# A hybrid decoder layer: the out-projection's rank in the schedule, and half buffers for its transposed rows

## The chip, the cores and the metric

The kernel runs on one core of one Trainium2 chip. The metric is the device time of one execution in microseconds (us). The kernel before was timed in three runs; one more execution was taken with the hardware profiler.

## The reference, cut to what matters

One decoder layer works on 2048 prompt rows and 64 sample rows (eight sequences of eight) of width 1024, all sharing the weights:

```python
proj = x @ w_in                       # columns split among three mixers
oa = gated_delta_chunked(...)         # mixer A, 6 heads, chunks of 64
ob = rg_lru(...)                      # mixer B, width 256
oc, gla_new = gla_chunked(qc, kc, vc, logf, st_gla)   # mixer C, 6 heads, chunks of 64
oc = head_rms_norm(oc, norm_c_w) * silu(zc)
heads = concatenate([oa, ob, oc], -1)
x = layer_norm(ALPHA * x + heads @ w_out, ln1_g, ln1_b)
f, fconv_new = conv_ffn(x, st_fconv, ffn_w_up, ffn_conv_w, ffn_conv_b, ffn_w_down)
x = layer_norm(ALPHA * x + f, ln2_g, ln2_b)
```

The change lies where mixer C, the product with `w_out` and the first layer norm are computed.

## The kernel before, in words

The program has four stages. `phase1` computes the columns of `x @ w_in` and stores them in DRAM; `window_a` runs mixer A; `window_c` runs mixer C and the out-projection; `phase3` is the feed-forward part. Products in full precision are made from three products of split operands (`mm3`, line 320): high by high, low by high, high by low.

`window_c` walks over nine groups: the sample rows first (`G[8]`), then eight groups of 256 prompt rows. For each it calls:

- `load` (L1276, L1279): the group's decays, keys, queries and values, on SP's queue. It is called one group ahead.
- `prep`: `natural` and `tokens` make scaled copies and transposes; then for each of six heads `fill` lays out the keys and queries (copies on ACT at L1349 to L1362, 36 small DMAs K<-KN in all for a group on SP's queue at L1351 and L1359, products on GpSimd at L1353 and L1363), and `scores` multiplies them (L1374) and gathers the result in `RC` (a copy at L1377 for the first level, then masked copies at L1380).
- `chain`: four chunks in sequence. Each has state products into `cs` (L1428, copied by L1437 into the next chunk's state) and output products into `po` (L1431). After two chunks `head_norm` turns `po` into the last three rows of `mx`, the heads of a tile of 128 rows. `dest` gets `mx` and the tile's `x` by DMA (L1511, L1513).
- for each tile of 128 rows, the projection `P(t0)`: split `mx` into `mh` (ACT, L1525) and `ml` (GpSimd, L1526), 48 matmuls with `woh` and `wol` into two `pm` banks (L320), `ALPHA * x` added (L1532), layer norm (L1171 to L1186), store of the rows to `s_x1` (L1537). Then `P.transposed` with `keep=1`: for the tile before, eight transposes into two `pm` banks (L1550), two copies into `xt` (ACT, L1551), a store of `xt` to `s_x1T` (SP, L1553).

The sample group has a second half: `sample` reads the eight GLA states into four buffers that `spare()` borrows from the projection's pool, and updates and stores them (L1447 to L1469). Between its two halves `P.weights` loads `w_out` in eight pieces through the ring `x` (L1495) and splits them into `woh` (ACT, L1496) and `wol` (DVE and GpSimd in turn, L1497).

The buffers that couple the two kinds of work: `mx` has two slots, `x` three, `mh`, `ml` and `xt` one each, the `pm` banks two (shared by projection and transposes), the `po` banks two. `RC`, `XC` and `KC` alternate between two groups; fills go through three sets of slots.

The order on each engine in `window_c` is not written out by hand. A scheduler takes the instructions in the order in which the program traces them as their rank, and a ready instruction of better rank goes first. `tc.high_priority(n)` moves the rank of what is in it by `n` places; a negative number is a setback. In the kernel before, `P` and `P.transposed` are set back by 100,000, more than there are instructions in the stage. `phase3` has an order written out by hand; its buffers take the place of those of `window_c`, and it reads `x1T0` (prompt rows up to 1023) first, five of eight pieces by GpSimd's queue and three by SP's (L1667).

Of the kernel before, what the change touches and what calls it, by code (L numbers as in the profile page):

```python
# [8 lines left out]
F32 = mybir.dt.float32  # L9
# [7 lines left out]
T = 2048  # L17
# [4 lines left out]
KD = DM // 128  # L22
# [281 lines left out]
def load_consts(E, pool, names):  # L304
    t = {}
    for n in names:
        o, w = _CST[n]
        t[n] = pool.tile([128, w], F32, name="c_" + n)
        E.nc.sync.dma_start(t[n], E.d["consts"][:, o:o + w])
    return t  # L310
# [1166 lines left out]
class Project:  # L1477
# [21 lines left out]

    def spare(self):  # L1500

        tags = [("mx", 2), ("mh", 1), ("ml", 1), ("xt", 1)]
        return [self.tr.tile([128, 2, 6, 64], F32, tag=t, bufs=b, name="sp" + t) for t, b in tags]

    def dest(self, t0):
# [34 lines left out]
    def transposed(self, ident, keep=0):  # L1540

        E, nc = self.E, self.E.nc
        while len(self.done) > keep:
            t0, m, x = self.done.pop(0)
            xt = self.tr.tile([128, KD, 128], F32, tag="xt", bufs=1, name=f"xt{t0}")
            for j in range(2):
                p = self.pm.tile([128, 4, 128], F32, tag="pm", name=f"pt{t0}{j}")
                for k in range(4):
                    kk = 4 * j + k
                    nc.tensor.transpose(p[:, k], x[:, kk * 128:(kk + 1) * 128], ident)  # L1550
                nc.scalar.copy(xt[:, 4 * j:4 * j + 4], p)  # L1551
            b, o = divmod(t0, 1024) if t0 < T else (1, t0 - 1024)
            nc.sync.dma_start(E.s[f"x1T{b}"].rearrange("(k p) t -> p k t", p=128)[:, :, o:o + m], xt[:, :, :m])  # L1553


def window_c(E):

    with ExitStack() as ctx:
        C = Gla(E, ctx)
        P = Project(E, ctx)  # L1560
        C.C.update(load_consts(E, ctx.enter_context(E.tc.tile_pool(name="c3", bufs=1)), ["ident", "ones"]))
        room = P.spare()
        C.dest = P.dest
        order = [C.G[8]] + C.G[:8]
        C.load(order[0])
        for i, g in enumerate(order):
            if i < 8:
                C.load(order[i + 1])
            C.prep(g)
            if g.smp:  # L1570
                smp = C.sample(g, room)
                next(smp)
                P.weights()
            else:
                if g.g == 0:
                    next(smp)
                C.chain(g)
            for t0 in range(g.t0, g.t0 + g.n, 128):
                with E.tc.high_priority(-10 ** 5):
                    P(t0)  # L1580
                    P.transposed(C.C["ident"], 1)
        P.transposed(C.C["ident"])
# [373 lines left out]
def program(tc, dram):  # L1956

    E = Env()
    E.nc, E.tc, E.d = tc.nc, tc, dram
    with ExitStack() as ctx:  # L1960
        setup(E, ctx)
        phase1(E)
        window_a(E)
        window_c(E)
        phase3(E)
# [16 lines left out]
```

## Time and profile before

| What | Value |
|---|---|
| median of three runs | 3042.56 us (3039.36 to 3044.3) |
| profiled execution, its own time | 3038.56 us |
| span of the profiled execution | 3036.8 us |
| PE busy | 2885.8 us (95%) |
| DVE, ACT, POOL busy | 1521.1, 1230.0, 847.7 us |
| mean granted TensorE clock | 0.954 |
| first score matmul of the sample group, about | 1010 us |
| first and last matmul of the projection | 1096.8 and 1506 us |
| first dense matmul of the feed-forward part | 1508 us |

The profile is one execution. A row of the timeline gives the start in us, the duration, the engine, the line, what is written and read, and how often; in brackets stands the idle time before it and what ended that. A row of a stretch gives busy time by engine, the granted clock of TensorE, the busy share of the DMA engines and GB/s. SPq is SP's queue, which issues almost all DMAs in their order.

### The profile page before, as it was taken

To read this page: it belongs to the slowest core of one execution; us is meant where nothing else is said; L and a number is where in the kernel's file an instruction comes from. 1 tells how busy PE (TensorE), PEld (TensorE's weight loads), DVE (VectorE), ACT (ScalarE), POOL (GpSimd) and SP (SyncE) were. 2 spreads that over 40 slices of the span, in tenths; PEclk is the share of its full clock that TensorE was granted. 3 is DMA by queue.
4 is the path that set the end of the run, shared out by engine and by line. 5 is a ranking of instruction groups with operands and counts; after the bars stand their busy time and mean duration, and the time that the engine had idled before them with its cause. 6 is when DMAs were issued, how large, how long until landed. Compare 5 with 4: busy or idle time off the path is not lost.

```text
span 3036.8 us, 45291 instructions
## 1 busy us (share of the span) xinstructions
PE 2885.8 (95%) x17755; PEld 2497.7 (82%) x17755; DVE 1521.1 (50%) x2454; ACT 1230.0 (41%) x2591; POOL 847.7 (28%) x904
## 2 busy tenths in 40 slices
PE   9999999789889889699899999999999999999998
PEld 8888789678879576577778888888889999999997
DVE  4564442586663777665633333333366444334446
ACT  4474443446653788844332222222232222222223
POOL 0000001734433555533332222222232222222224
PEclk9999999789889589799999999999999999999999
DMA  6221113433433443244531111111124111111111
GB/s 198 81 76 67 58 60 101 137 104 108 119 91 95 114 128 110 83 132 120 184 131 56 49 42 63 42 56 42 49 106 151 42 47 51 49 42 42 47 44 62
DMA packets 196508, 256.77 MB, mean 85 GB/s; under 512 B 43170, under 2 KB 162040, under 8 KB 196232
## 3 DMA queue, kind: packets, MB, share of 16 engines
q1 hardware_dynamic: 194168, 246.58, 26.2%
q0 software_dynamic: 1984, 7.12, 0.6%
q8 instruction: 140, 2.29, 0.3%
q14 instruction: 72, 0.59, 0.1%
q10 hardware_dynamic: 144, 0.20, 0.0%
HBM read 183.94 MB, written 60.08 MB: 80 GB/s over the span
## 4 chain that ended last, share of the span: by engine, by line
PE 78%; DVE 7%; ACT 6%; issue 4%; DMA 3%; POOL 2%; SPq 1%; POOLq 0%; DVEq 0%; ACTq 0%
PE pm L320 19%; PE pd L320 15%; PE pug L320 15%; PE puv L320 15%; PE s L1374 1%; PE zp L1121 1%; DVE Tm L897 1%; DVE y L1789 1%; PE zp L1122 1%; PE zp L1123 1%; ACT Q L1362 1%; ACT WU L920 1%; DVE tmp L895 1%; PE pd L1871 1%; PE cw L962 1%
## 5 line engine op out<-in xcount | busy, mean ns | idle before, releaser
L1725 DVE SCALAR_TENSOR_TENSOR act<-G,cols,act 128x1024 f32<-128x1024 f32 (+1 forms) x132 | 123.6, 951 | 493.0 <-ACT act L1723 490.7
L1878 DVE TENSOR_TENSOR y<-y,pd 128x512 f32<-128x512 f32 x322 | 221.0, 687 | 203.3 <-PE pd L320 196.8
L1616 POOL TENSOR_TENSOR wl_d<-ws_d,wh_d 128x1024 fp32r<-128x1024 f32 x44 | 106.2, 2414 | 571.4 <-ACT wh_d L1615 520.7
L320 PE MATMUL pd<-wh_d,hh 128*128 128x512 f32 x704 | 216.0, 392 | 2.7 <-DVE y L1876 1.8
L320 PE MATMUL pd<-wh_d,hl 128*128 128x512 f32 x704 | 215.3, 391 | 0.0
L320 PE MATMUL pd<-wl_d,hh 128*128 128x512 f32 x704 | 214.9, 390 | 0.0
L1705 ACT COPY G<-pug 128x512 f32<-128x512 f32 (+2 forms) x110 | 55.0, 501 | 386.5 <-PE pug L320 386.5
L320 PE MATMUL pug<-fxh,wh_g 128*128 128x512 f32 (+2 forms) x880 | 196.3, 352 | 2.6 <-ACT wh_g L1615 2.6
L320 PE MATMUL puv<-fxh,wh_v 128*128 128x512 f32 (+2 forms) x880 | 197.2, 353 | 0.8 <-ACT wh_v L1615 0.8
L320 PE MATMUL puv<-fxh,wl_v 128*128 128x512 f32 (+2 forms) x880 | 196.9, 352 | 0.7 <-POOL wl_v L1616 0.7
L320 PE MATMUL puv<-fxl,wh_v 128*128 128x512 f32 (+2 forms) x880 | 196.7, 352 | 0.0
L320 PE MATMUL pug<-fxh,wl_g 128*128 128x512 f32 (+2 forms) x880 | 195.9, 351 | 0.4 <-POOL wl_g L1616 0.4
L320 PE MATMUL pug<-fxl,wh_g 128*128 128x512 f32 (+2 forms) x880 | 195.8, 351 | 0.0
L320 PE MATMUL pm<-xh,wh 128*128 128x448 f32 (+1 forms) x800 | 181.9, 360 | 6.6 <-ACT xh L370 6.4
L1615 ACT CAST wh_d<-ws_d 128x1024 fp32r<-128x1024 f32 x44 | 45.7, 1040 | 339.1 <-PE pd L1871 174.9
L320 PE MATMUL pm<-xh,wl 128*128 128x448 f32 (+1 forms) x800 | 181.5, 358 | 0.0
L320 PE MATMUL pm<-xl,wh 128*128 128x448 f32 (+1 forms) x800 | 179.9, 358 | 0.5 <-DVE xl L371 0.5
L1767 DVE TENSOR_TENSOR hl<-act,hh 128x512 fp32r<-128x512 f32 (+2 forms) x110 | 124.1, 1128 | 99.4 <-ACT hh L1759 99.4
L320 PEld LDWEIGHTS pug<-fxh,wh_g 128*128 128x128 f32 x880 | 156.0, 188 | 17.5 <-ACT wh_g L1615 3.0
L320 PEld LDWEIGHTS puv<-fxh,wh_v 128*128 128x128 f32 x880 | 156.4, 188 | 15.1 <-ACT wh_v L1615 1.2
L320 PEld LDWEIGHTS puv<-fxh,wl_v 128*128 128x128 f32 x880 | 156.1, 188 | 15.0 <-POOL wl_v L1616 1.1
L320 PEld LDWEIGHTS puv<-fxl,wh_v 128*128 128x128 f32 x880 | 156.0, 188 | 13.9
(731 smaller groups left out, 6264.0 us busy)
## 6 DMA issues: line engine op xcount, KB each, us to landing
ws_d<-in_w_dn SPq DMA_DIRECT2D x44, 512.0 KB
ws_g<-in_w_up SPq DMA_DIRECT2D x43, 512.0 KB
ws_v<-in_w_up SPq DMA_DIRECT2D x43, 512.0 KB
zx<-in_xT SPq DMA_DIRECT2D x56, 256.0 KB
ws<-in_w_in SPq DMA_DIRECT2D x19, 512.0 KB
K<-KN SPq DMA_DIRECT2D x288, 32.0 KB
x<-in_x SPq DMA_DIRECT2D x16, 512.0 KB
s_x<-x SPq DMA_DIRECT2D x16, 512.0 KB
```

The lines of the kernel that those rows point to most:

```text
L320: nc.tensor.matmul(ps, w[k], x[k], start=first and i == 0, stop=last and i == 3 * n - 1)
L895: nc.vector.tensor_tensor(t, Y[:, j + 1:, j:j + 1].to_broadcast([128, k, j + 1]), Tm[:, j:j + 1, :j + 1].to_broadcast([128, k, j + 1]), op ...
L897: nc.vector.tensor_tensor(Tm[:, j + 1:, :j + 1], Tm[:, j + 1:, :j + 1], t, op=OP.subtract)
L920: nc.scalar.copy(o[:, h, :, :, jh * 32:(jh + 1) * 32], Ut[r, :, :3 * mt].rearrange("p i (a c) -> p a c i", a=3)[:, :, g.c0:g.c0 + m])
L962: nc.tensor.matmul(ps[64:, h], g.WU[:, h, c], g.X[:, h, c], start=True, stop=True)
L1121: nc.tensor.matmul(ps, wh[:, k], xl, start=k == 0, stop=False)
L1615: nc.scalar.copy(h, t)
L1616: nc.gpsimd.tensor_tensor(lo, t, h.bitcast(F32), op=OP.subtract)
L1705: nc.scalar.copy(G[:, 2 + o:2 + o + m], p[:, :m])
L1725: nc.vector.scalar_tensor_tensor(dst(act), src(i), taps[i], dst(act), op0=OP.mult, op1=OP.add)
L1767: nc.vector.tensor_tensor(dst, act[:, c], hh[:, c].bitcast(F32), op=OP.subtract)
L1878: nc.vector.tensor_tensor(y, y, ps, op=OP.add)
```

## The change

It does three things. The setback of `P` and `P.transposed` goes from 100,000 places to 600. `xt` becomes two half buffers of four blocks each (the pool's default of two buffers), and each half is stored by a DMA of its own right after its copy. `spare()` takes its fourth buffer from the ring `x` (three slots), as the old `xt` is no more.

```diff
     def spare(self):
-        tags = [("mx", 2), ("mh", 1), ("ml", 1), ("xt", 1)]
+        tags = [("mx", 2), ("mh", 1), ("ml", 1), ("x", 3)]
         return [self.tr.tile([128, 2, 6, 64], F32, tag=t, bufs=b, name="sp" + t) for t, b in tags]
...
         while len(self.done) > keep:
             t0, m, x = self.done.pop(0)
-            xt = self.tr.tile([128, KD, 128], F32, tag="xt", bufs=1, name=f"xt{t0}")
+            b, o = divmod(t0, 1024) if t0 < T else (1, t0 - 1024)
             for j in range(2):
+                xt = self.tr.tile([128, 4, 128], F32, tag="xt", name=f"xt{t0}{j}")
                 p = self.pm.tile([128, 4, 128], F32, tag="pm", name=f"pt{t0}{j}")
                 for k in range(4):
                     kk = 4 * j + k
                     nc.tensor.transpose(p[:, k], x[:, kk * 128:(kk + 1) * 128], ident)
-                nc.scalar.copy(xt[:, 4 * j:4 * j + 4], p)
-            b, o = divmod(t0, 1024) if t0 < T else (1, t0 - 1024)
-            nc.sync.dma_start(E.s[f"x1T{b}"].rearrange("(k p) t -> p k t", p=128)[:, :, o:o + m], xt[:, :, :m])
+                nc.scalar.copy(xt, p)
+                nc.sync.dma_start(E.s[f"x1T{b}"].rearrange("(k p) t -> p k t", p=128)[:, 4 * j:4 * j + 4, o:o + m],
+                                  xt[:, :, :m])
...
             for t0 in range(g.t0, g.t0 + g.n, 128):
-                with E.tc.high_priority(-10 ** 5):
+                with E.tc.high_priority(-600):
                     P(t0)
                     P.transposed(C.C["ident"], 1)
         P.transposed(C.C["ident"])
```

## The prediction

> **What bounds the kernel now.** I read the page first (span, chain), then the busy time by stretches of the stage that the change touches, then the timelines of PE, SP and ACT inside the one stretch that looked wrong.
>
> ```profile
> span 3036.8 us, 45291 instructions
> PE 78%; DVE 7%; ACT 6%; issue 4%; DMA 3%; POOL 2%; SPq 1%; POOLq 0%; DVEq 0%; ACTq 0%
> ```
>
> The chain that ends last is TensorE for 78%. A change of order can only help where PE stands still, so I cut the stage of the change (1097 to 1508 us: GLA groups and projection together) into stretches. The columns are PE, PEld, DVE, ACT, POOL busy, then the granted clock.
>
> ```profile
> 1100.00:1220.00 120.00, 112.15 (x1055) 86.98 (x1054) 88.29 (x187) 99.74 (x305) 67.12 (x114) 1.00 0.37 103
> 1220.00:1280.00 60.00, 40.51 (x419) 33.67 (x416) 40.40 (x105) 52.42 (x169) 34.22 (x83) 0.75 0.27 72
> 1280.00:1290.00 10.00, 0.01 (x1) 0.01 (x1) 2.31 (x6) 3.88 (x18) 3.68 (x7) 0.50 0.45 139
> 1290.00:1508.00 218.00, 211.08 (x1347) 166.94 (x1348) 129.71 (x174) 96.22 (x226) 68.45 (x82) 0.98 0.45 139
> ```
>
> Before 1220 PE is busy 112.15 of 120 us (93%) at full clock, after 1290 it is busy 211.08 of 218 (97%). Between lies a hole of 70 us with 40.5 us of PE work at a clock of 0.75 and 0.50. The next rows show why.
>
> ```profile
> 1216.51 0.60 PE L1550 MATMUL pt<-c_ident,x 128*128 128x128 f32 x4
> 1289.99 3.78 PE L320 MATMUL pm<-woh,mh 128*128 128x512 f32 x8 [11.80 <-ACT xt L1551]
> 1191.56 0.58 ACT L1551 COPY xt<-pt 128x512 f32<-128x512 f32 x1
> 1289.35 1.07 ACT L1551 COPY xt<-pt 128x512 f32<-128x512 f32 x2 [3.76 <-DMA s_x1T<-xt]
> 1283.38 2.44 SPq L1351 DMA_DIRECT2D K<-KN  x4
> 1285.88 0.58 SPq L1553 DMA_DIRECT2D s_x1T<-xt  x1
> ```
>
> The second half of one tile's `xt` was copied at 1191.56, yet its store was issued at 1285.88, 94 us later, behind K loads (L1351, L1359) on SP's queue. `xt` is one buffer, so the next tile's transposes, done at 1216.51 into both `pm` banks, could not be copied out before 1289.35. With both banks taken no projection matmul could run. What is left at 1290 shows in the same stretch for the matmuls on `woh` alone:
>
> ```profile
> 1290.00:1508.00 218.00, 110.09 (x416) 79.47 (x416) 0.00 (x0) 0.00 (x0) 0.00 (x0) 0.98 0.45 139
> ```
>
> A tile has 32 of them, so 416 are thirteen of the seventeen tiles, and PE is the bound until they are done. So projection work that moves into the hole shortens the stage almost one for one.
>
> **The change part by part.**
>
> *The rank.* Counting instructions in the code, a group has 397 of its own (load 7, natural 64, tokens 32, six heads of fill and scores at 36, chain 78) and two tiles of projection 144. A setback of 600 puts the projection of group g 59 places behind the same point of group g+1: behind all of g+1's work, ahead of g+2's fills. Today's setback of 100,000 puts it behind everything. The K loads that overtook the store in the hole are fills of later groups; those two or more groups later now rank behind it. I cost the rank as filling the hole. The room in it: the 40.5 us run at a low clock, and the same eight score matmuls show the price of that.
>
> ```profile
> 1209.67 0.68 PE L1374 MATMUL s<-Q,K 128*64 128x64 f32 x8
> 1236.18 1.08 PE L1374 MATMUL s<-Q,K 128*64 128x64 f32 x8 [2.12 <-POOL Q L1353]
> ```
>
> At 0.68 against 1.08 the hole's work is 40.5 x 0.63 = 25.5 us at full clock, so 70 - 25.5 = 44.5 us are free; with the low clock kept it is 29.5. I take 44.5, since a stretch that holds both kinds of work had clock 1.00, and 93% of it, as in 1100 to 1220: **41 us gained** (bounds 27 to 44.5). One tile in lockstep takes
>
> ```profile
> 1435.87 3.96 PE L320 MATMUL pm<-woh,mh 128*128 128x512 f32 x16
> 1448.15 0.92 PE L1431 MATMUL po<-RC,XC 128*64 128x64 f32 x24
> 1449.45 3.94 PE L320 MATMUL pm<-woh,mh 128*128 128x512 f32 x16
> ```
>
> 1449.45 - 1435.87 = 13.6 us, so three tiles move. Their other instructions move with them. On ACT these are the split, two copies and two small ones:
>
> ```profile
> L1525 ACT CAST mh<-mx x17: 1027/1046/1049, 1094.8 to 1493.5; 128x1024 fp32r<-128x1024 f32 x17
> 1402.77 0.22 ACT L1179 ACTIVATE mv<-mv 128x1 f32<-128x1 f32 x1
> ```
>
> 1.05 + 2 x 0.58 + 2 x 0.22 = 2.6 us a tile, against 13.7 us idle in the hole (70 - 52.4 - 3.9); on DVE and POOL similar shares. These engines come close to full there, so fills slip to after 1290, where ACT is busy only 96 of 218 us: this cover makes it free. SP: three x1 stores, three x1T stores and their waits now stand between K loads. SP has room when PE is the bound:
>
> ```profile
> SPq L1513 <- PE pt L1550: 49.1, 12, 13.5
> ACT xt L1551 <- DMA s_x1T<-xt: 10.0, 2, 6.2
> ```
>
> SP itself sat 49.1 us waiting for transposes to free an `x` buffer. What waits behind such a wait are K loads, and behind those the scores of a later group, which is not what bounds the stage while PE has projection to do. I put it at 0.
>
> *Two half buffers.* The bytes are the same (two of 2 KB a partition for one of 4 KB). A half is stored right after its own copy, and a copy waits for the store two halves back. The gain is at most the 10.0 us that ACT waited here in two waits, of which 3.76 lie in the hole and are counted above. The cost is 17 more issues on SP at 0.58 (row of 1285.88), 9.9 us in 411, on a queue with 49.1 us of waits: between -10 and +10, taken as 0. The Trainium skill (DMA: Bandwidth & Descriptors, Bandwidth) speaks against it: batch transfers to 1 MiB and more; here 512 KB becomes twice 256 KB. Its section on the anatomy of one DMA gives a fixed cost of about 2.0 us each, for the GpSimd path; if 17 of these lay on the path, the sum would be an estimated 34 us worse by that page. Today's rows show only two waits for such a store, so I keep 0.
>
> *The spare.* `spare()` hands the sample's fourth state buffer a slot of the `x` ring (three) where it had `xt`. The sample tile's own `x` holds the second until its transposes. The staging of `w_out` (L1495 to L1498, same ring) falls from two slots to one.
>
> ```profile
> 1054.96 1.04 ACT L1496 CAST woh<-wos 128x1024 fp32r<-128x1024 f32 x1 [1.67 <-DMA K<-KN]
> 1072.61 0.81 SPq L1495 DMA_DIRECT2D wos<-in_w_out  x2
> 1078.65 1.04 ACT L1496 CAST woh<-wos 128x1024 fp32r<-128x1024 f32 x1
> 1079.73 1.22 DVE L1497 TENSOR_TENSOR wol<-wos,woh 128x1024 fp32r<-128x1024 f32 x1
> 1081.52 0.53 SPq L1495 DMA_DIRECT2D wos<-in_w_out  x1
> 1082.90 2.42 POOL L1497 TENSOR_TENSOR wol<-wos,woh 128x1024 fp32r<-128x1024 f32 x1
> 1085.34 0.35 SPq L1495 DMA_DIRECT2D wos<-in_w_out  x1
> 1092.56 1.04 ACT L1496 CAST woh<-wos 128x1024 fp32r<-128x1024 f32 x1
> 1106.57 0.35 SPq L1469 DMA_DIRECT2D o_glas<-spxt  x1
> ```
>
> A slot's round is 1081.52 - 1072.61 = 8.9 us with DVE's subtraction, up to 12.3 with POOL's (the other slot, about 1073.0 to 1085.34). Eight rows in one slot: last cast at 1055 + 7 x 8.9 = 1117, at worst 1055 + 7 x 12.3 = 1141, instead of 1092.56; the spare returns its slot after 1106.57 and cuts the worse end. So the weights come some 25 us later. What PE loses is the projection that it did in that time:
>
> ```profile
> 1080.00:1100.00 20.00, 3.20 (x9) 2.60 (x10) 0.74 0.57 163
> 1100.00:1120.00 20.00, 10.31 (x41) 7.00 (x39) 1.00 0.39 106
> 1120.00:1140.00 20.00, 3.94 (x16) 2.92 (x16) 1.00 0.27 72
> ```
>
> (L320 alone.) 3.2 + 10.3 = **13.5 us lost**; bounds 0 (PE caught up in its later 7% idle) to 17.5 (to 1140). Queued behind a staging load that waits for its slot on SP are K loads and the `mx` and `z` loads of groups 0 and 1.
>
> *The end of the stage.* The FFN's buffers lie where the groups' rings lay. After the last `po` (1448.15) SP loads FFN weights, and the fifth split of the FFN's input ends at 1487.6:
>
> ```profile
> 1449.12 0.34 SPq L1607 DMA_DIRECT2D ws_g<-in_w_up  x1
> 1484.78 2.78 POOL L1669 TENSOR_TENSOR fxl<-fxl,fxh 128x1024 fp32r<-128x1024 f32 x1 [0.56 <-ACT fxh L1668]
> ```
>
> That is 38.5 us from the end of `po`. Four tiles (54 us) cover it today. With n left the cost is 38.5 - 13.6 n: 0 for three or four, 11 for two. The rings (two `mx`, two `po` banks) still let chains lead by four tiles, so I take **3 us**.
>
> Sum: 41 - 13.5 - 3 = 24.5 us gained. The profiled execution has 3038.56 us around its span of 3036.8 and would come to 3014; it is 4.0 below the median 3042.56 of the three runs, so the median forecast is **3018**. By its own terms: best 44.5 - 0 - 0 = 44.5, worst 27 - 17.5 - 11 = -1.5.
>
> **The rivals.**
>
> 1. *Alternation (slower).* Where the projection outranks group g+2's prep, PE may take two tiles in a row while the score matmuls wait, the three K/Q slots fill up, and ACT stops. Prep and projection then add instead of overlapping. In the hole, prep alone ran at four heads in 20 us:
>
> ```profile
> 1240.00:1260.00 20.00, 1.47 (x4) 0.83 0.29 79
> ```
>
> (L1377, one copy a head.) Six heads are 30 us; with two tiles 30 + 27.2 = 57.2 us a group, against 411/8 = 51.4 today. Eight groups: 46 us slower if nothing overlaps; it decides as soon as less than 6 us of each group's 27.2 overlap. Half of that, +23, gives 3066. Against it: 1100 to 1220 mixed both at 93%.
>
> 2. *The hole only moves.* Another single buffer (`mh`, `ml`), the `x` ring or SP holds the projection up the same way, and the late weights remain. -6 to +14 us, 3044 in the middle. For it: `mh` and `ml` are single too; against it: those are freed by PE, not by a queue. That the new rank leaves the order in the hole as it was belongs here.
>
> 3. *The stores come onto the path.* Each half waits for its landing, 1289.35 - 1285.88 = 3.5 us: if the 17 added ones do so in line, +59, less the 24.5: about 3077. The page rule above would give 34 - 24.5 = 10 us slower as an estimate. Two waits in 34 copies speak against it.
>
> 4. *The end is bare.* One tile or none left at the last `po`: 25 or 38.5 us idle in place of 3, so -2.5 to +11 net, 3047. For it: the projection is now done earlier; against it: the ring lead.
>
> **How the numbers follow.** Forecast 0.62; rivals 0.14, 0.12, 0.03, 0.09. A measurement of this kernel tells about 0.2%, 6 us, from no change. The forecast's own range is 2998 to 3044. The range reaches over rivals 2 and 4 (3056) and leaves out most of 1 and 3 and the forecast's far end: **2998 to 3056**. Faster by over 0.2%: 0.59 of the forecast, 0.02 of rival 2, 0.04 of rival 4: 0.65. Within 0.2%: 0.02 + 0.06 + 0.04 = 0.12. Slower: 0.23.
>
> **What would show it.** Right: no 20 us stretch between 1140 and the stage's end with PE under 17 busy or clock under 0.9; x1T stores issued within some 10 us of their copy; the last `woh` cast near 1117; the last projection matmul near 1483 (1508 - 24.5) in place of 1506. The spare is wrong if that cast stays near 1093; the end is wrong if PE idles over 10 us between last `pm` and dense `pug`. The forecast fails if projection waits for ACT's or SP's turn again, or if score matmuls wait for `pm` tiles in every group.

## The result, and the profile after

| | before | after |
|---|---|---|
| median of four runs each | 3043.19 us (3039.36 to 3044.3) | 3005.86 us (3003.07 to 3010.3) |
| ratio, 95% interval | | 0.9881 (0.9864 to 0.9898) |
| profiled execution, span | 3038.56, 3036.8 us | 3003.07, 3001.3 us |

The ratio is 36 us of gain (31 to 41); 24.5 were forecast. (Here and below, us from a ratio are one minus the ratio, times the median of before that was taken beside it.) One execution below, the profiled one of the kernel with all stores raised but one, took 5544 us where the ten others took 3036 to 3043; it is in no ratio, and only the order of its instructions is used. The line of the span and that of the chain, on the page of the changed kernel:

```profile
span 3001.3 us, 45267 instructions
PE 61%; DVE 4%; ACT 2%; issue 1%; POOL 1%; DMA 1%; SPq 0%; DVEq 0%; POOLq 0%; ACTq 0%
```

PE's share of the chain fell from 78% to 61% although PE now idles less. The chain is one path followed back, and its shares add up to only 70% here; it is not the measure of what bounds the kernel. The stretches are. The same columns as in the prediction (PE, PEld, DVE, ACT, POOL busy, granted clock), changed kernel:

```profile
1100.00:1220.00 120.00, 111.18 (x907) 86.13 (x905) 90.94 (x183) 92.20 (x276) 66.18 (x102) 0.96 0.45 130
1220.00:1290.00 70.00, 68.48 (x565) 52.94 (x566) 50.24 (x95) 54.95 (x160) 37.64 (x65) 1.00 0.47 136
1290.00:1473.00 183.00, 177.85 (x1329) 139.00 (x1328) 121.76 (x199) 108.95 (x282) 79.87 (x120) 1.00 0.45 139
```

The hole is gone: 68.48 us of PE work in the 70 us that held 40.5. ACT's copies and SP's stores around the same time in the changed kernel (the second tile's two halves):

```profile
1207.36 0.59 ACT L1552 COPY xt<-pt 128x512 f32<-128x512 f32 x1
1207.97 0.38 SPq L1553 DMA_DIRECT2D s_x1T<-xt  x1
1211.72 0.59 ACT L1552 COPY xt<-pt 128x512 f32<-128x512 f32 x1
```

A store follows its copy at once. To see what the whole stage gained, and what the end behind it did, cut the span at the last projection matmul. First before, then after:

```profile
1100.00:1506.32 406.32, 362.74 (x2809) 286.83 (x2808) 259.10 (x469) 251.67 (x713) 173.47 (x285) 0.94 0.40 119
```

```profile
1100.00:1471.36 371.36, 356.54 (x2788) 277.35 (x2787) 261.46 (x472) 255.51 (x716) 183.69 (x286) 0.99 0.46 136
```

From there to the end of the span it is 3036.8 - 1506.3 = 1530.5 us before and 3001.3 - 1471.4 = 1529.9 after. All the gain lies ahead of the last projection matmul, and most of it is idle time of PE: 406.3 - 362.7 = 43.6 us before, 14.8 after.

### The profile page after: what moved, and what is told of

Read it like the earlier page. It is cut to its first block, busy times and chain, and to the rows that moved or that the text cites. A ratio compares the mean times of both kernels' runs of the same rounds, so it can differ in the third digit from the quotient of the medians.

```text
span 3001.3 us, 45267 instructions
## 1 busy us (share of the span) xinstructions
PE 2877.8 (96%) x17755; PEld 2484.7 (83%) x17755; DVE 1514.8 (50%) x2454; ACT 1230.8 (41%) x2591; POOL 854.8 (28%) x904
## 4 chain that ended last, share of the span: by engine, by line
PE 61%; DVE 4%; ACT 2%; issue 1%; POOL 1%; DMA 1%; SPq 0%; DVEq 0%; POOLq 0%; ACTq 0%
PE pug L320 16%; PE pd L320 16%; PE puv L320 15%; PE pm L320 6%; PE s L1374 2%; DVE y L1791 1%; PE pd L1873 1%; PE cs L1428 1%; PE zp L1121 1%; POOL Q L1353 1%; PE po L1431 0%; PE po L1206 0%; ACT Q L1362 0%; PE pv L1395 0%; PE zp L1123 0%
## 5 line engine op out<-in xcount | busy, mean ns | idle before, releaser
L320 PE MATMUL pd<-wh_d,hh 128*128 128x512 f32 x704 | 215.2, 390 | 3.4 <-DVE y L1878 1.8
L320 PE MATMUL pd<-wh_d,hl 128*128 128x512 f32 x704 | 214.8, 390 | 0.0
L320 PE MATMUL pd<-wl_d,hh 128*128 128x512 f32 x704 | 214.5, 389 | 0.0
L320 PE MATMUL pug<-fxh,wh_g 128*128 128x512 f32 (+2 forms) x880 | 196.6, 352 | 2.6 <-ACT wh_g L1617 2.6
L320 PE MATMUL puv<-fxh,wh_v 128*128 128x512 f32 (+2 forms) x880 | 196.9, 352 | 0.9 <-ACT wh_v L1617 0.9
L320 PE MATMUL pug<-fxh,wl_g 128*128 128x512 f32 (+2 forms) x880 | 197.0, 353 | 0.0
L320 PE MATMUL puv<-fxh,wl_v 128*128 128x512 f32 (+2 forms) x880 | 196.6, 352 | 0.2 <-POOL wl_v L1618 0.2
L320 PE MATMUL puv<-fxl,wh_v 128*128 128x512 f32 (+2 forms) x880 | 196.5, 352 | 0.0
L320 PE MATMUL pug<-fxl,wh_g 128*128 128x512 f32 (+2 forms) x880 | 196.0, 351 | 0.0
L320 PE MATMUL pm<-xh,wh 128*128 128x448 f32 (+1 forms) x800 | 181.9, 360 | 7.2 <-ACT xh L370 6.3
L320 PE MATMUL pm<-xh,wl 128*128 128x448 f32 (+1 forms) x800 | 181.8, 359 | 0.0
L320 PE MATMUL pm<-xl,wh 128*128 128x448 f32 (+1 forms) x800 | 180.2, 358 | 0.2 <-DVE xl L371 0.2
L320 PEld LDWEIGHTS pug<-fxh,wh_g 128*128 128x128 f32 x880 | 156.0, 188 | 17.5 <-ACT wh_g L1617 3.0
L320 PEld LDWEIGHTS puv<-fxh,wh_v 128*128 128x128 f32 x880 | 156.2, 188 | 15.2 <-ACT wh_v L1617 1.3
L320 PEld LDWEIGHTS pug<-fxh,wl_g 128*128 128x128 f32 x880 | 156.2, 189 | 14.7 <-POOL wl_g L1618 0.7
L320 PEld LDWEIGHTS puv<-fxh,wl_v 128*128 128x128 f32 x880 | 155.9, 188 | 14.5 <-POOL wl_v L1618 0.6
```

The costliest lines, as they stand in the source:

```text
L320: nc.tensor.matmul(ps, w[k], x[k], start=first and i == 0, stop=last and i == 3 * n - 1)
```

## What was to be told apart

The time answers the question whether, not the question why. The change has three parts, and the prediction gave the whole gain to one of them. The theories at the start:

- **A, the rank does it** (the prediction): the projection's instructions must outrank the K loads of groups that come later. The halves are worth 0, the spare costs 13.5 us.
- **B, the half buffers do it**: one whole `xt` blocks the transposes whatever the rank.
- **C, one queue**: the hole is a late store on SP's queue, and only the store's place matters.

After the first four runs came **D**: the hole hangs on one place in the written order, the store of the tile at `t0 = 0`, and an edit that moves that place forward removes it.

Every kernel was timed four to eleven times, beside the kernel before on the same chip. The kernels were taken in three batches on three chips, so kernels of different batches are compared by their ratios.

| kernel | median, us | ratio to before, 95% | gain, us |
|---|---|---|---|
| rank alone (`e1_rank`) | 3011.07 | 0.9907 (0.9892 to 0.9922) | 28 |
| rank and spare (`e5_rank_spx`) | 3007.87 | 0.9899 (0.9882 to 0.9915) | 31 |
| halves and spare, old rank (`e2_halves`) | 3001.41 | 0.9874 (0.9859 to 0.9889) | 38 |
| stores' rank alone (`e3_store`) | 3006.28 | 0.9892 (0.9877 to 0.9907) | 33 |
| spare alone (`e6_spare_only`) | 3011.35 | 0.9905 (0.9890 to 0.9920) | 29 |
| two stores alone (`e7_two_stores`) | 3040.84 | 1.0002 (0.9993 to 1.0011) | -1 |
| store on ACT's queue (`e8_act_store`) | 3008.76 | 0.9897 (0.9883 to 0.9910) | 31 |
| changed, rank 0 (`e9_rank0`) | 3034.15 | 0.9984 (0.9975 to 0.9993) | 5 |
| one store's rank (`e10_one_store`) | 3010.08 | 0.9905 (0.9892 to 0.9919) | 29 |
| all stores' but that one (`e13_all_but_one`) | 3039.91 | 0.9999 (0.9990 to 1.0008) | 0 |
| halves, stores on ACT (`e11_halves_act`) | 3000.96 | 0.9876 (0.9860 to 0.9892) | 38 |
| changed, rank 1200 (`e12_rank1200`) | 3005.01 | 0.9887 (0.9874 to 0.9901) | 34 |

## Experiments: the parts one by one

**Rank alone.** Against the kernel before:

```diff
-                with E.tc.high_priority(-10 ** 5):
+                with E.tc.high_priority(-600):
```

> The kernel before with the new rank alone (setback 600 in place of 100,000; one whole xt, the spare still in xt, so the weights are staged through two slots as before). Theory A (the rank does it: SP takes the x1T store ahead of the loads of later groups, and projection fills the hole): the hole at 1220 to 1290 is gone, the last woh cast stays near 1093, and the time is that of the changed kernel less what the spare costs there: between 2992 (spare costs 13.5) and 3006 us (costs nothing). Theory B (a single xt holds the transposes up whatever the rank; the two halves are what helps): a hole of 40 us or more stays somewhere between 1140 and 1480, the time is 3025 to 3043 us.

3011.07 us: 5 us above A's range, far from B's. The hole is gone without half buffers, so B falls as the only cause. The same stretch, rank alone:

```profile
1220.00:1290.00 70.00, 66.47 (x536) 51.36 (x534) 51.94 (x100) 54.18 (x162) 37.14 (x59) 1.00 0.46 137
```

**Rank and spare.** As before this one, and

```diff
-        tags = [("mx", 2), ("mh", 1), ("ml", 1), ("xt", 1)]
+        tags = [("mx", 2), ("mh", 1), ("ml", 1), ("x", 3)]
```

> The new rank, and the spare in the x ring as in the changed kernel, but one whole xt with one store a tile. Beside the rank-only kernel it has only the spare's place, beside the changed kernel only the halves. The prediction's terms: spare +13.5 us (last woh cast near 1120 in place of 1093), halves 0 (-10 to +10): so 13.5 us above the rank-only kernel and within 10 of 3006. The rival reading of the changed kernel's trace (the weights come 30 us later, but PE has caught up by 1140): spare 0 to 4 us, so the two ranks kernels agree within 0.2%. If the halves matter, this one is over 6 us above 3006.

3007.87, 3 us below the rank alone, intervals overlapping, and 2 us above the changed kernel by the medians, 5 by the ratios: the halves don't show here. The spare's mechanism is there and its price is not. The casts of `w_out` and the matmuls of L320 alone, first with the rank alone, then with rank and spare (a row of the matmuls has PE and PEld busy, then the clock):

```profile
L1496 ACT CAST woh<-wos x8: 1044/1044/1047, 1058.0 to 1096.3; 128x1024 fp32r<-128x1024 f32 x8
...
1080.00:1100.00 20.00, 0.00 (x0) 0.00 (x0) 0.76 0.60 180
1100.00:1120.00 20.00, 14.10 (x48) 10.54 (x48) 0.86 0.42 118
1120.00:1140.00 20.00, 0.00 (x0) 0.00 (x0) 1.00 0.29 79
```

```profile
L1496 ACT CAST woh<-wos x8: 1027/1028/1046, 1056.1 to 1120.9; 128x1024 fp32r<-128x1024 f32 x8
...
1080.00:1100.00 20.00, 3.54 (x10) 2.28 (x10) 0.81 0.49 134
1100.00:1120.00 20.00, 1.47 (x4) 0.60 (x4) 0.93 0.61 175
1120.00:1140.00 20.00, 12.70 (x50) 9.16 (x50) 0.92 0.38 105
```

The last cast comes 24.6 us later (1120.9 against 1096.3), as forecast. But by 1140 the kernel with late weights has done 17.7 us of projection and the other 14.1: what could not be done at 1100 was done at 1120, in time that had no other projection to do.

**Halves and spare at the old rank.** The changed kernel with `high_priority(-10 ** 5)` again.

> The changed kernel with the old setback of 100,000: half buffers, two stores and the spare in the x ring, but not the new rank. Theory A (the rank does it): the stores still come late behind K loads, a hole of tens of us with PE under 17 in 20 us and clock under 0.9 stays, and the time is 3035 to 3060 us (3043 before, up to 10 either way for the halves, 0 to 13.5 worse for the weights). Theory B (the halves do it): no such hole, 3006 to 3020 us.

3001.41: A falls in its strict form. Without the new rank the time is as good as with it (0.9874 against 0.9881), and 5 us below the range of theory B too. And the stores are late here. Copies on ACT and stores on SP, halves at the old rank:

```profile
1187.13 1.08 ACT L1552 COPY xt<-pt 128x512 f32<-128x512 f32 x2
...
1206.39 0.43 SPq L1553 DMA_DIRECT2D s_x1T<-xt  x1
1220.13 0.58 SPq L1553 DMA_DIRECT2D s_x1T<-xt  x1
```

The second tile's halves wait some 19 and 32 us for their stores (both copies done by 1188.2), where one store waited 94 us before. Stores that are late by this much did no harm that the time shows.

**The stores' rank alone.** The kernel before, with the store at the rank of its own place:

```diff
-            nc.sync.dma_start(E.s[f"x1T{b}"]...[:, :, o:o + m], xt[:, :, :m])
+            with E.tc.high_priority(10 ** 5):
+                nc.sync.dma_start(E.s[f"x1T{b}"]...[:, :, o:o + m], xt[:, :, :m])
```

> The kernel before with only the x1T store taken out of the setback: it has the rank of its place in the program, all other projection work stays set back by 100,000. Theory C (the hole is one late store on SP's queue): the store follows its copy within some 10 us, the hole is gone, and the time is within 8 us of the kernel with the new rank alone, 3000 to 3015 us. Theory A in its wide form (all of the projection's instructions have to outrank later groups' work, the x1 stores, loads and copies too): the hole comes back at another place, 3030 to 3043 us.

3006.28: C holds. The 17 stores moved in SP's order give what the whole change gives, within the intervals.

At this point three different edits had each removed the hole, one of them with rank and queue as before. Hence D, and the runs that follow.

**Spare alone.** The kernel before with only the `spare()` line of above.

> The kernel before with the spare in the x ring as the only edit: old setback of 100,000, one whole xt, one store a tile. Theory D (the hole is an accident of the order: once the projection falls behind, the K loads fill SP's queue and the store of lowest rank never gets a turn; anything that shifts the moments of the first tiles avoids it): the weights come 25 us later, the second tile's store falls into a moment when SP is free, the hole is gone, 3000 to 3012 us. Theory B (the two half buffers made the gain of the kernel with halves at the old rank) and the prediction's term (the spare costs 13.5 and nothing else): the hole stays, 3040 to 3057 us.

3011.35: 29 us faster, from the part that the prediction had priced at 13.5 us of loss. The second tile's copies and store, spare alone, and the stretch:

```profile
1193.61 1.07 ACT L1551 COPY xt<-pt 128x512 f32<-128x512 f32 x2
...
1211.64 1.22 SPq L1553 DMA_DIRECT2D s_x1T<-xt  x1
```

```profile
1220.00:1290.00 70.00, 67.56 (x568) 52.42 (x568) 51.40 (x107) 53.98 (x160) 42.12 (x70) 1.00 0.45 131
```

The store is 17 us late, not 94, at the lowest rank, after copies only 2 to 3 us later than in the kernel before (1191.56). The edit had shifted the order of the stage, and in the new one the store got another place on SP: behind 160 K loads, counted from the first of the stage, where it was behind 250 in the kernel before.

**Two stores alone.** The whole single `xt`, each half stored after its copy:

```diff
                 nc.scalar.copy(xt[:, 4 * j:4 * j + 4], p)
+                nc.sync.dma_start(E.s[f"x1T{b}"]...[:, 4 * j:4 * j + 4, o:o + m], xt[:, 4 * j:4 * j + 4, :m])
-            nc.sync.dma_start(E.s[f"x1T{b}"]...[:, :, o:o + m], xt[:, :, :m])
```

> The kernel before with the tile's store cut in two, each right after its own copy, from the one whole xt; rank, buffer and spare as before. Theory D: the first tiles' moments do not shift, both stores of the second tile wait behind the K loads, the hole stays and with it 3033 to 3050 us (17 more issues on SP are worth up to 10 us). A theory that the finer stores helped: hole gone, 3000 to 3015 us.

1.0002: nothing. The hole is where it was. Copy, stores and stretch with two stores alone:

```profile
1195.91 0.57 ACT L1552 COPY xt<-pt 128x512 f32<-128x512 f32 x1
...
1289.27 1.38 SPq L1553 DMA_DIRECT2D s_x1T<-xt  x2
```

```profile
1220.00:1290.00 70.00, 45.38 (x479) 37.67 (x478) 47.35 (x118) 59.46 (x196) 41.17 (x93) 0.74 0.26 69
```

Both stores of that tile now wait some 94 us, behind the same 250 K loads. The run also prices 17 added issues on SP and their fixed costs: -2 to +3 us, with the late store still behind as many K loads. By the fixed cost of about 2.0 us that the Trainium skill (DMA: Bandwidth & Descriptors, Anatomy of one DMA) gives for the GpSimd path, 17 in line would have been an estimated 34 us; the time shows that they did not lie on the path.

**The store on ACT's queue.** `nc.scalar.dma_start` in place of `nc.sync.dma_start` for the x1T store of the kernel before, old rank.

> The kernel before with the x1T store issued by ACT's queue in place of SP's, at its old rank; all else as before. If what made the hole is SP's queue full of K loads (theories C and D), the store follows its copy at once, the hole is gone, 3000 to 3012 us. If it is the rank of the whole projection, on whatever queue (theory A in its wide form), a hole of 20 us or more stays and the time is above 3025 us.

3008.76, 31 us faster. The stretch, store on ACT's queue:

```profile
1220.00:1290.00 70.00, 66.33 (x574) 51.27 (x572) 54.22 (x109) 56.55 (x169) 38.66 (x68) 1.00 0.48 143
```

So it is the store's place on SP's queue, not the rank as such.

## Experiments: one store, and the ranks

**One store.** The kernel before, with one DMA of 17 moved:

```diff
-            nc.sync.dma_start(E.s[f"x1T{b}"]...[:, :, o:o + m], xt[:, :, :m])
+            with E.tc.high_priority(10 ** 5 if t0 == 0 else 0):
+                nc.sync.dma_start(E.s[f"x1T{b}"]...[:, :, o:o + m], xt[:, :, :m])
```

> The kernel before with one DMA alone taken out of the setback: the x1T store of the tile at t0 = 0, the second tile of the stage, which was issued 94 us after its copy. The other 16 stores and all else keep the old rank. If the hole hangs on this one store (theory D), it is gone and the time is that of the kernel with all stores raised, 3000 to 3012 us. If each tile's store is late in its turn (theory A in its wide form), the hole moves to a later tile and the time stays above 3030 us.

**All stores but that one.** The same line with the two numbers exchanged (`0 if t0 == 0 else 10 ** 5`).

> The reverse: all x1T stores at the rank of their place, but for the one of the tile at t0 = 0, which keeps the setback of 100,000. Theory D: the hole at 1220 to 1290 stays as it was, 3035 to 3046 us. If the general rank of the stores makes the gain, at least half of it shows: below 3025 us.

0.9905 and 0.9999. One DMA raised takes 29 us off (25 to 33); the sixteen others raised take off nothing. Copy, store and stretch with one store raised:

```profile
1195.33 0.57 ACT L1551 COPY xt<-pt 128x512 f32<-128x512 f32 x1
...
1195.92 0.46 SPq L1554 DMA_DIRECT2D s_x1T<-xt  x1
```

```profile
1220.00:1290.00 70.00, 68.14 (x579) 52.96 (x578) 48.59 (x107) 57.00 (x169) 40.36 (x70) 1.00 0.49 143
```

The profile of the second kernel (all stores raised but that one) is the execution of 5544 us. Its times can't be compared, but the order in which SP issues can. SP's K loads ahead of the store of `t0 = 0`, in the kernel before and in that one:

```profile
L1351 SPq DMA_DIRECT2D K<-KN x160: 507/542/1534, 1002.2 to 1285.2; - x160
L1359 SPq DMA_DIRECT2D K<-KN x90: 507/562/1734, 989.7 to 1282.7; - x90
```

```profile
L1351 SPq DMA_DIRECT2D K<-KN x160: 507/542/2247, 1701.0 to 2066.6; - x160
L1359 SPq DMA_DIRECT2D K<-KN x90: 507/578/1718, 1685.1 to 2064.0; - x90
```

250 both times, and 250 with two stores alone. Where the hole is gone it is fewer: 149 with one store raised, 150 in the changed kernel, 160 with the spare alone and with the halves. So the late store is a matter of its place in the order that was written before the run. SP keeps to that order: in the kernel before it waited 4.7 us with a load of `z` (issued at 1232.5) for DVE (L1210), while the data of the store had been ready since 1192.

How the place could come about is suggested by SP's K loads from 1243 to 1286. First before, then after (shortest, median and longest ns of an issue, first and last start):

```profile
L1351 SPq DMA_DIRECT2D K<-KN x40: 507/542/1534, 1243.7 to 1285.2; - x40
L1359 SPq DMA_DIRECT2D K<-KN x18: 512/541/652, 1246.2 to 1282.7; - x18
```

```profile
L1351 SPq DMA_DIRECT2D K<-KN x22: 507/542/1217, 1243.5 to 1285.4; - x22
L1359 SPq DMA_DIRECT2D K<-KN x10: 507/518/863, 1244.7 to 1281.9; - x10
```

58 K loads in 43 us against 32. In the kernel before these and six other loads take 39.9 of the 42.2 us ahead of the store. With PE free of projection, the groups' preparation ran in these 43 us about as fast as SP could issue, at 0.54 us each and more. If the scheduler reckons so too, it has a K load of better rank for SP at every moment, and the state keeps itself up: no store, hence no projection, hence fast preparation, hence a full queue, hence no store. That loop is argued, not shown.

**Rank 0.** The changed kernel with `high_priority(0)`.

> The changed kernel with a setback of 0 in place of 600: the projection of a group ranks ahead of all work of the next group. Rival 1 of the prediction (alternation: two tiles run through while the scores wait and preparation and projection add instead of overlapping) gives the changed kernel +23 to +46 us when it decides: here, where it should be stronger, PE would be under 17 of 20 us in most of the stretches between 1140 and 1400, and the time 3029 to 3052 us. If PE stays the bound at any rank (there is always prepared work of one kind), 3001 to 3012 us, the same as at 600.

3034.15: rival 1 of the prediction is real, 28 us above the changed kernel by the medians, at the rank where it had to be strongest. Four stretches with rank 0, then PE inside one of them:

```profile
1220.00:1240.00 20.00, 15.05 (x131) 11.32 (x132) 14.48 (x33) 18.86 (x53) 12.36 (x24) 0.91 0.20 54
...
1280.00:1300.00 20.00, 15.52 (x101) 11.38 (x100) 16.96 (x44) 19.30 (x59) 13.17 (x22) 0.74 0.27 74
1300.00:1320.00 20.00, 20.00 (x131) 16.14 (x130) 10.83 (x18) 8.18 (x26) 6.92 (x10) 1.00 0.50 152
1320.00:1340.00 20.00, 16.23 (x166) 12.71 (x165) 11.65 (x19) 14.58 (x42) 12.03 (x22) 0.87 0.36 106
```

```profile
1287.16 1.09 PE L1374 MATMUL s<-Q,K 128*64 128x64 f32 x8 [0.88 <-POOL Q L1353]
1289.45 1.09 PE L1374 MATMUL s<-Q,K 128*64 128x64 f32 x8 [1.21 <-POOL Q L1353]
...
1294.86 3.94 PE L320 MATMUL pm<-woh,mh 128*128 128x512 f32 x16
```

ACT is full (19.30 of 20) while PE waits for the next head, then PE is full of projection while ACT has 8.18. The two kinds of work take turns. It was expected in most stretches between 1140 and 1400; PE is under 17 in four of the thirteen, about once a group. From 1100 to the last projection matmul PE idles 37.6 us, against 14.8 in the changed kernel.

**Rank 1200, and the halves with ACT's queue.** The changed kernel with `high_priority(-1200)`; the halves at the old rank with `nc.scalar.dma_start` for the x1T stores.

> The changed kernel with a setback of 1200 in place of 600: a group's projection ranks behind two to three later groups. Rank 0 gave 3034, rank 600 3006, rank 100,000 3001 us. If the half buffers and the shifted start alone do it and a rank of 600 already costs some alternation, this one lies at 3000 to 3005; if 600 is the right distance and longer ones lose, above 3006 us.

> The best so far (the changed kernel's half buffers, two stores and spare at the old setback of 100,000: 3001) with the stores issued by ACT's queue. If stores that wait 10 to 30 us in SP's queue still cost PE something there, some us faster: 2993 to 2999. If the stores are no longer on any path, the same within 0.2%, 2996 to 3008; if the 34 issues cost ACT its turn, slower, up to 3015 us.

3005.01 and 3000.96. Ranks 600, 1200 and 100,000 (0.9881, 0.9887, 0.9874) can't be told apart, so the first of the two gives no verdict between its readings. The second is the same as with SP's queue (0.9876 against 0.9874): with half buffers, stores that wait up to 32 us cost nothing that these intervals (some 5 us either way) can show. No version is shown to beat the changed kernel.

## Why the prediction was right, and where it was not

The direction, the place and the mechanism of the hole were right: one late store on SP, a single `xt`, two `pm` banks held. The total came out 12 us short, with errors of both signs in the terms. The two large ones, 13 us too much for the rank and 13.5 of loss for the spare, cancel, and that is luck.

- **The rank, +41 forecast, 28 measured alone (24 to 33).** The hole filled better than assumed (68.5 of 70 us, not 93%), but it was smaller: the step that failed is 40.5 x 0.63 = 25.5 us, the hole's work "at full clock". With one store moved, the hole holds 68.14 - 40.51 = 27.6 us more PE work, and after it 29.3 us less remain. PE until its last projection matmul, from 1290, before and with one store raised:

```profile
1290.00:1506.32 216.32, 210.07 (x1340) 166.17 (x1341) 128.10 (x171) 95.63 (x225) 68.45 (x82) 0.98 0.45 140
```

```profile
1290.00:1477.68 187.68, 180.74 (x1236) 140.10 (x1235) 116.70 (x179) 97.97 (x251) 76.19 (x105) 0.98 0.46 142
```

  By this balance the hole's 40.5 us stood for 68.1 - 29.3 = 38.8 us of work, not 25.5, and the room was the idle 29.5 on which the prediction had its lower bound. One row of eight matmuls at two clocks was taken for the whole stretch. The low clock did cost something: the hole's 296 score matmuls took 30.11 us, 0.102 us each, against 0.080 for the other 648 before 1506, 6.5 us in all and not 15. That was not gained either: the projection's matmuls took 6.9 us more in the kernel with one store raised (last section). Nor did ACT come close to full in the hole, as the prediction had it: 54.95 of 70 us in the changed kernel.
- **That the rank was the cause** is the step that failed in kind. It removes the hole, and so do the spare alone, the stores' rank alone and ACT's queue. The parts do not add: 28 and 29 us for two of them alone are the same hole, 31 together.
- **The spare, -13.5 forecast, 0 measured** (3 us better beside the rank, intervals overlapping). The late weights came about when forecast (last cast at 1122.1 in the changed kernel, 1117 forecast); the price was wrong. It took projection that was done later for projection that was lost. Alone, the same edit gained 29 us by moving the store. The bound of 0, "PE caught up", was the right end.
- **The halves, 0 forecast (-10 to +10).** Beside the spare alone they gain 9 us (0.9874 against 0.9905, in two batches; the intervals end at 0.9889 and begin at 0.9890); beside rank and spare 5, not to be told from none. Where these come from is open: from 1100 to its last projection matmul PE idles 22.3 us with the spare alone and 14.9 with the halves, and is busy 6.5 us less. The two rows, in that order:

```profile
1100.00:1480.18 380.18, 357.92 (x2778) 277.93 (x2778) 261.38 (x471) 254.62 (x714) 183.80 (x286) 0.97 0.44 133
```

```profile
1100.00:1466.31 366.31, 351.45 (x2751) 272.93 (x2749) 261.06 (x465) 252.42 (x706) 182.56 (x280) 0.99 0.45 136
```

- **The end, -3 forecast, 0 measured** (1530.5 against 1529.9 us behind the last projection matmul). Three tiles covered it, as the prediction allowed. Rival 4 is out.
- **The sum.** 29 for the hole, 0 for the spare, 5 to 9 for the halves, 0 for the end: 34 to 38, against 36 measured. The halves' 5 to 9 is the term that is not shown.
- **The other rivals.** 1 does not decide at 600 and does at 0. 2 (whose middle, between -6 and +14, is 3047 and not 3044) and 3 are out: no other buffer took the hole's place, and ACT waited for stores 5.9 us in two waits (10.0 before).
- **The marks.** Met: stores within 10 us of their copies, and the late casts. The last projection matmul ended at 1471.4, not 1483. One mark was too strict: the stretch 1160 to 1180 has PE 16.81 at clock 0.91.

Open is why the scheduler put the store of `t0 = 0` behind 250 K loads in one order and behind 160 in another, at the same lowest rank. No trace shows what the scheduler had to choose from.

## What to carry to other kernels

When a lowest-ranked instruction shares an in-order queue with work that its own lateness speeds up, it can be starved for as long as that work lasts (argued here, not shown); look for the one instruction whose buffer holds the others, and move that. Test the parts of a change alone before crediting one of them: where all remove the same stall, their gains do not add, and a part that looks like a cost may remove it too. Price delayed work at what is still missing when the queue of such work next runs dry, not at what was missing in the first window.

## What was not expected of the hardware

- **A full queue beside idle DMA engines.** In the kernel before, SP issued nearly without a pause from 1243 to 1286, a median of 0.54 us for a K load, while the DMA engines were 26% busy. The Trainium skill (DMA: Bandwidth & Descriptors, Rules for kernel authors) says that spreading DMAs over the issuing engines saves only the sequencer's issue time. Here it was worth more: the issues of the 17 stores are 6.3 us on SP (17 x 0.37, the median in the kernel before), and moving them to ACT's queue gained 31. That gain is the place in SP's order, since one store raised on SP's own queue gives 29.
- **PE's busy time under a low clock.** From 1100 to the last projection matmul PE was busy 362.74 us before, at a mean granted clock of 0.94, and 361.73 us with one store moved, at 0.98. That row of the second:

```profile
1100.00:1477.68 377.68, 361.73 (x2816) 280.56 (x2815) 253.49 (x476) 252.32 (x716) 183.15 (x288) 0.98 0.44 129
```

  The equal sums hide two differences that cancel. The score matmuls (L1374) alone, before and with one store moved:

```profile
1100.00:1506.32 406.32, 81.71 (x944) 68.85 (x944) 0.94 0.40 119
```

```profile
1100.00:1477.68 377.68, 75.23 (x944) 62.39 (x944) 0.98 0.44 129
```

  They took 6.5 us more in the kernel with the low clock. The projection's 816 matmuls took less there, 209.38 us against 216.30 from 1090 on (sums by line overlap in part). Why they take longer with one store moved, no run here shows. So a sum of busy time can stay the same while its parts move.
